# Up projection of a gated FFN: pairs of weight units against groups of four

## The chip, the core and the metric

The kernel runs on one core of one Trainium2 chip. The metric is device microseconds (us) of one execution. The kernel before takes 755.76 us, the median of three runs (755.01 to 755.77). All durations below come from one further execution that was recorded by the profiler; it took 755.7 us, of which 753.9 us lie between its first and its last instruction (the span). So 1.8 us lie around the span.

Engines are named as in the profile: PE does matrix products (PEld is its weight load), DVE is the vector engine, ACT the activation engine, POOL the general one, SP the queue that issues the transfers here. Each engine works through its own list of instructions in the order of the program.

## The reference, cut to what matters

Two decoder layers over 256 positions of width 1024. Each layer is an attention mixer followed by a gated feed-forward net (FFN) with a causal convolution of width 3:

```python
def conv_ffn(h, w_up, conv_w, conv_b, w_down):
    u = h @ w_up                                   # (256, 1024) @ (1024, 2 * 2816)
    up = jnp.pad(u, ((0, 0), (CONV_WIDTH - 1, 0), (0, 0)))
    uc = conv_b + sum(conv_w[j] * up[:, j:j + S] for j in range(CONV_WIDTH))
    gate, val = uc[..., :D_FF], uc[..., D_FF:]
    return (jax.nn.silu(gate) * val) @ w_down      # (256, 2816) @ (2816, 1024)
```

## The kernel before, in words

**Split numbers.** A product of 32-bit numbers is made of three products of rounded parts: high times high, high times rest, rest times high. Weights arrive as `raw` tiles. `Stream.start` has ACT write the high part (`whi`, L111), `Stream.finish` has DVE write the rest (`wlo`, L119). There are 6 `raw` buffers and 8 pairs of `whi` and `wlo`. A `raw` tile is loaded again (L83, on SP) once DVE has written the rest of the tile that held it; a pair of parts is written again once its unit was released (`Stream.release`) and PE is done with it.

**Units of the FFN.** 2816 gate columns and 2816 value columns are cut into blocks of 128. A block pair f (1 to 10; pair 0 is done apart by `first_up`) has four up units of 1024x128 weights: gate j=0 with e=0, 1, then value j=1 with e=0, 1. Below they are called f.1 to f.4. Each has 8 slices k.

**Up projection (`up`).** `xT[:, k]` holds, side by side, the high part and the rest of the input, 256 columns each. A wide product (L950) multiplies a slice of `whi` with all 512 columns; a narrow one (L968) multiplies the slice of `wlo` with the 256 high columns and adds to the second half. Per unit there are 8 wide and 8 narrow ones, all into one 128x512 accumulator, which fills a bank. Four banks rotate over the units (three named `acc`, one named `O`), so that a unit takes the bank of the unit four before it. In the kernel before, a pair of units (one j) is one piece of work: the first unit's 8 wide products, the second's first wide product, 8 narrow and 8 narrow, the second's other 7 wide.

**After a unit.** `join` adds the two halves of the accumulator: ACT copies the second half (L979), DVE adds it to the first and writes the sum to `sm` (L980). The bank is free once that addition has been made. `conv` makes the convolution of two joined units: two operations on ACT (L988), four on DVE (L991). For the gate a SiLU follows on ACT (L230 in the profile); for the value, DVE multiplies (L999), ACT takes the high part (`parts_of`, L1004) and DVE the rest (L230 on DVE).

**Down projection (`downs`).** A down unit b of 128x1024 weights takes 12 products of 128x512 (L1020 to L1022). Down units 2f-4 and 2f-3 are placed by `downs_after(f)`, from f=2 to f=9; six more come at the end of the FFN (`tail`).

**Turns.** `turn(fn)` writes one stretch of the program for all engines: up to two `start`s, then what is due under `first` (joins, SiLU, parts), one `finish`, what is due under `pre` (convolutions), the other `finish`es, then PE's work `fn`, then what is due under `post`. A join is due in the turn after its unit's, a gate's or value's convolution in the turn after its second unit's. Pair 0's convolutions are due one and three turns after the last `first_up` (`flip`, L932 to L940).

Of the kernel before, what the change touches and what calls it, by code (L numbers as in the profile page):

```python
# [10 lines left out]
F32 = mybir.dt.float32  # L11
# [6 lines left out]
P = 128  # L18
D = 1024
S = 256  # L20
# [123 lines left out]
def trunk_kernel(ctx, tc, x, a_w_qkv, a_w_o, b_w_qkv, b_w_o, ffn_norm, ffn_w_up, ffn_w_down, pack, mask_a, mask_b,  # L144
                 x_t, out):
    nc = tc.nc
    cp = ctx.enter_context(tc.tile_pool(name="cp", bufs=1))
    wp = ctx.enter_context(tc.tile_pool(name="wp", bufs=1))
    bp = ctx.enter_context(tc.tile_pool(name="bp", bufs=1))
# [5 lines left out]
    def qkv_cols(w, k0, nk, c0, n, stride):  # L155
        row = w.shape[1]
        return bass.AP(tensor=w.tensor, offset=w.offset + k0 * P * row + c0,
                       ap=[[row, P], [P * row, nk], [stride, n], [1, SW]])

    def qkv_units(w, ng):  # L160
        h3 = ng * NH * HD
        for sec in range(NSEC):
            opening = ng == 3 and sec == 0
            if opening:

                yield from (bass.AP(tensor=w.tensor, offset=w.offset + k * P * w.shape[1],
                                    ap=[[w.shape[1], P], [NH * HD, 2], [h3, 2], [1, SW]]) for k in range(8))
            for g in range(2 if opening else 0, ng):
                c0 = g * NH * HD + sec * SW
                yield from (qkv_cols(w, 2 * u, 2, c0, 2, h3) for u in range(4))  # L170
            c0 = 2 * h3 + sec * SW
            if ng == 3:
                yield from (qkv_cols(w, 2 * u, 2, c0, 2, NH * HD) for u in range(4))
                c0 += 2 * NH * HD

            if sec in V_TURN[ng]:
                yield from (qkv_cols(w, 2 * u, 2, 2 * h3 + (2 * NH * HD if ng == 3 else 0) + sec // 2 * 2 * SW, 2, SW)
                            for u in range(4))

    def out_units(w):  # L180
        wv = w.rearrange("(k p) n -> p k n", p=P)
        for n, u in OUT_UNITS:
            yield wv[:, 2 * u:2 * u + 2, n * 512:(n + 1) * 512]

    NPAIR = NFB // 2
    NT = 3

    def downs_after(f, j, e):

        bs = (2 * f - 4, 2 * f - 3)  # L190
        if not e or f not in range(2, NPAIR - NT + 2):
            return ()

        return bs[j:j + 1] if f > 2 else bs if j else ()

    def ffn_units(l):
        wu = ffn_w_up[l].rearrange("(k p) n -> p k n", p=P)
        wd = ffn_w_down[l].rearrange("(b p) n -> p b n", p=P)
        yield from (qkv_cols(ffn_w_up[l], 2 * u, 2, 0, 2, DFF) for u in range(4))
        for f in range(1, NPAIR):  # L200
            for j in range(2):
                for e in range(2):
                    c0 = j * DFF + (2 * f + e) * P
                    yield wu[:, :, c0:c0 + P]
                    for b in downs_after(f, j, e):
                        yield wd[:, b, :]
        for b in range(NFB - 2 * NT, NFB):
            yield wd[:, b, :]

    ws = Stream(nc, wp, [u for l, (q, ng, o) in enumerate(((a_w_qkv[0], NG, a_w_o[0]), (b_w_qkv[0], 1, b_w_o[0])))  # L210
                         for it in (qkv_units(q, ng), out_units(o), ffn_units(l)) for u in it])


    now = [0]
    first, pre, mid, post = {}, {}, {}, {}

    def at(table, dt, fn, *args):
        table.setdefault(now[0] + dt, []).append((fn, args))

    def turn(fn, pump=2, crowded=False):  # L220

        t = now[0]
        end = len(ws.parts) if t >= LATE else None
        n = min(pump, 1 if len(ws.parts) - ws.taken >= AHEAD else 2)
        if not crowded:
            ws.start(n)
        if t - 1 in EARLY_TURNS:
            ws.finish()
        for f, a in first.pop(t, ()):
            f(*a)  # L230
        ws.finish(1, end)
        for f, a in pre.pop(t, ()):
            f(*a)
        if crowded:
            ws.start(n)
        ws.finish(end=end)
        if fn is not None:
            fn()

        if t in EARLY_TURNS:  # L240
            ws.start(2)
        late = post.pop(t, [])
        part = PART[t >= PART_TURNS]
        late.sort(key=lambda fa: part.get(fa[0].__name__, len(part)))
        for f, a in late:
            f(*a)
        now[0] += 1
# [210 lines left out]
    def new_T():  # L458
        return cp.tile([P, 8, 2, S], F32R, name="xT", bufs=2)

    def new_acc():
        return ps.tile([P, 512], F32, name="acc", bufs=3)
# [439 lines left out]
    def ffn(xT, l, end):  # L902
# [41 lines left out]
        def up_bank():  # L944
            banks[0] += 1
            return ps.tile([P, 512], F32, name="O", bufs=1) if banks[0] % 4 == 2 else new_acc()

        def wide(acc, hi, ks):
            for k in ks:
                nc.tensor.matmul(acc, hi[:, k], xT[:, k].rearrange("p j t -> p (j t)"),  # L950
                                 start=(k == 0), stop=(k == 7 and ks[0] == 1))

        def up(f, j, e, st):


            def go():
                unit, = ws.take(1)
                if e == 0:
                    st["t"] = bp.tile([P, 512], F32, name="qk", bufs=5)
                    st["acc"] = bp.tile([P, 768], F32, name="sm", bufs=2)[:, 0:512]  # L960
                    st["up"] = up_bank(), up_bank()
                acc = st["up"][e]
                _, hi, lo = unit
                if e == 0:
                    wide(acc, hi, range(8))
                    wide(st["up"][1], ws.parts[ws.taken][0], range(1))
                for k in range(8):
                    nc.tensor.matmul(acc[:, S:2 * S], lo[:, k], xT[:, k, 0], start=False, stop=(k == 7 and e == 0))  # L968
                if e == 1:
                    wide(acc, hi, range(1, 8))  # L970
                ws.release(unit)
                at(first, 1, join, e, acc, st)
                if e == 1:
                    at(first if f == NPAIR - 1 and j else pre, 1, conv, f, j, st)
            return go

        def join(e, acc, st):
            small = bp.tile([P, 768], F32, name="pT", bufs=4)[:, 0:S]
# [31 lines left out]
        def down(b, c, ns=(0, 1), piece=None):  # L1010
            f, e = divmod(b, 2)
            cs = slice(e * S + c * P, e * S + (c + 1) * P)
            if not dacc:
                dacc.extend([ps.tile([P, 512], F32, name="S", bufs=4) for _ in range(2)] for _ in range(2))
            if b not in dw:
                dw[b] = ws.take(1)[0]
            _, hi, lo = dw[b]
            pieces = [(dacc[c][n], slice(n * 512, (n + 1) * 512), b == 0, b == NFB - 1 or (l, c, n, b) == PAUSE) for n in ns]
            for o, sl, start, stop in [piece] if piece else pieces:
                nc.tensor.matmul(o, acts[f][:, 0, cs], hi[:, sl], start=start, stop=False)  # L1020
                nc.tensor.matmul(o, acts[f][:, 1, cs], hi[:, sl], start=False, stop=False)  # L1021
                nc.tensor.matmul(o, acts[f][:, 0, cs], lo[:, sl], start=False, stop=stop)  # L1022
            if c == 1 and ns and ns[-1] == 1:
                ws.release(dw[b])

        def downs(b):
            def go():
                for c in range(2):
                    down(b, c)
            return go  # L1030
# [2 lines left out]
            for j in range(2):  # L1033
                turn(first_up(c, j), c + j)
        for f in range(1, NPAIR):
            for j in range(2):
                st = {}
                for e in range(2):
                    turn(up(f, j, e, st), 2)
                    for b in downs_after(f, j, e):  # L1040
                        turn(downs(b))
        rest = list(range(NFB - 2 * NT, NFB))

        def tail(c, bs, ns):
# [33 lines left out]
    xT = new_T()  # L1078
# [29 lines left out]
    xT = new_T()  # L1108
# [4 lines left out]
    def end0(c, n, acc):  # L1113
# [3 lines left out]
        if n == 1:  # L1117
            norms2[c].scale()
            if c == 0:
                at(post, 1, ready, norms2[0])  # L1120

    ffn(xT, 0, end0)


# [3 lines left out]
    xT = new_T()  # L1128
    out_proj(1, aT, xT)

    def end1(c, n, acc, c0=None):
# [3 lines left out]
        nc.sync.dma_start(out[0, c * P:(c + 1) * P, sl], xr[:, c, sl])  # L1135

    ffn(xT, 1, end1)


# [77 lines left out]
```

## Time and profile before

| what | value |
|---|---|
| median of three runs | 755.76 us |
| profiled execution, and its span | 755.7 us, 753.9 us |
| PE busy | 749.5 us, 99% of the span |
| DVE busy | 582.0 us, 77% |
| ACT busy | 506.4 us, 67% |
| POOL busy | 81.4 us, 11% |
| wide products (L950) | 640, into `acc` 118.8 us, into `O` 43.3 us |
| narrow products (L968) | 640, into `acc` 63.8 us, into `O` 22.6 us |
| rests of weights on DVE (L119) | 236, 283.8 us, 1218 ns each |
| high parts of weights on ACT (L111) | 236, 244.4 us, 1055 ns each |

Products are pipelined: the duration of one is longer than the time to the start of the next. So the pace of PE is read from starts. On DVE and ACT, too, the next operation may begin some 0.08 to 0.1 us before the former has ended, and lists are summed from start to start. The up projections of the first layer's pairs begin at 282.49 us, those of the second at 578.71 us.

### The profile page before, as it was taken

Reading aid. Unit: us, or ns where it says so; the run is one execution under the profiler, and the core shown is the slowest. Engines: PE = TensorE matmul, PEld = TensorE weight load, DVE = VectorE, ACT = ScalarE, POOL = GpSimd, SP = SyncE. Lnnn points to the kernel's source line nnn. Section 1 sums busy time; section 2 is a strip of 40 time slices with the busy share of each in tenths; the row PEclk is TensorE's granted clock in tenths of the full one; section 3 lists DMA queues with packets and bytes.
Section 4 is the critical chain, followed back from the end, with each engine's and each line's share of the span. In section 5 each row is a group of like instructions: output and inputs, shape, how many; then the busy total and the mean of one; then the engine's idle time right before and its main releaser. Section 6 shows DMA issues by size and latency. Waiting matters only on the chain.

```text
span 753.9 us, 12147 instructions
## 1 busy us (share of the span) xinstructions
PE 749.5 (99%) x4394; PEld 633.1 (84%) x4394; DVE 582.0 (77%) x1124; ACT 506.4 (67%) x887; POOL 81.4 (11%) x101
## 2 busy tenths in 40 slices
PE   9999999999999999999999999999999999999998
PEld 8888888888888888888888888888888888888886
DVE  7888786776686576997787786889866799877874
ACT  7878667677577457676656656787856667666660
POOL 0341331330131010000000001122000000000000
PEclk9999999999999999999999999999999999999999
DMA  9958576496456436587666663745545368666621
GB/s 294 333 145 285 158 259 233 149 294 219 132 194 230 128 94 201 152 249 217 195 188 181 194 193 113 250 140 155 161 136 166 112 198 243 201 185 197 194 95 56
DMA packets 151372, 141.69 MB, mean 188 GB/s; under 512 B 6288, under 2 KB 134928, under 8 KB 151312
## 3 DMA queue, kind: packets, MB, share of 16 engines
q1 hardware_dynamic: 148816, 130.96, 56.4%
q0 software_dynamic: 2496, 9.96, 3.5%
q8 instruction: 34, 0.56, 0.3%
q14 instruction: 26, 0.21, 0.1%
HBM read 131.99 MB, written 1.05 MB: 176 GB/s over the span
## 4 chain that ended last, share of the span: by engine, by line
PE 99%; DVE 0%; issue 0%
PE acc L950 15%; PE acc L467 13%; PE acc L469 13%; PE acc L468 13%; PE acc L968 8%; PE S L1021 5%; PE S L1022 5%; PE S L1020 5%; PE O L950 5%; PE O L968 3%; PE acc L524 2%; PE O L824 2%; PE S L791 2%; PE acc L600 1%; PE S L702 1%; PE S L469 1%
## 5 line engine op out<-in xcount | busy, mean ns | idle before, releaser
L119 DVE TENSOR_TENSOR wlo<-raw,whi 128x1024 fp32r<-128x1024 f32 x236 | 283.8, 1218 | 7.9 <-ACT whi L111 7.8
L111 ACT ACTIVATE whi<-raw 128x1024 fp32r<-128x1024 f32 x236 | 244.4, 1055 | 4.7 <-PE S L1021 1.4
L467 PE MATMUL acc<-whi,xT 128*128 128x512 f32 x424 | 171.1, 404 | 0.0
L469 PE MATMUL acc<-wlo,xT 128*128 128x512 f32 x424 | 165.6, 391 | 0.0
L468 PE MATMUL acc<-whi,xT 128*128 128x512 f32 x424 | 165.2, 390 | 0.0
L950 PE MATMUL acc<-xT,whi 128*128 128x512 f32 x480 | 118.8, 390 | 0.0
L950 PEld LDWEIGHTS acc<-xT,whi 128*128 128x128 f32 x480 | 88.8, 188 | 17.7
L469 PEld LDWEIGHTS acc<-wlo,xT 128*128 128x128 f32 x424 | 79.6, 188 | 17.3
L467 PEld LDWEIGHTS acc<-whi,xT 128*128 128x128 f32 x424 | 79.6, 188 | 15.9 <-issue 1.2
L468 PEld LDWEIGHTS acc<-whi,xT 128*128 128x128 f32 x424 | 79.8, 188 | 14.5
L1020 PE MATMUL S<-whi,kT 128*128 128x512 f32 x174 | 67.8, 390 | 0.0
L1021 PE MATMUL S<-whi,kT 128*128 128x512 f32 x174 | 67.8, 389 | 0.0
L1022 PE MATMUL S<-wlo,kT 128*128 128x512 f32 x174 | 67.7, 389 | 0.0
L327 POOL TENSOR_TENSOR rs_y<-rs_v,mhalf 128x8 f32<-128x8 f32 x32 | 53.1, 1659 | 128.1 <-DVE rs_v L325 128.1
L991 DVE SCALAR_TENSOR_TENSOR qk<-sm,taps,qk 128x255 f32<-128x255 f32 (+1 forms) x160 | 66.6, 477 | 0.4 <-ACT qk L988 0.4
L968 PEld LDWEIGHTS acc<-xT,wlo 128*128 128x128 f32 x480 | 62.9, 191 | 3.1
L968 PE MATMUL acc<-xT,wlo 128*128 128x256 f32 x480 | 63.8, 283 | 0.0
L980 DVE TENSOR_TENSOR sm<-acc,pT 128x256 f32<-128x256 f32 x60 | 25.4, 424 | 46.5 <-ACT pT L979 46.5
L988 ACT ACTIVATE qk<-sm,taps 128x256 f32<-128x256 f32 x80 | 47.9, 598 | 4.2 <-DVE sm L980 3.9
L950 PE MATMUL O<-xT,whi 128*128 128x512 f32 x160 | 43.3, 392 | 0.0
L1004 ACT ACTIVATE kT<-qk 128x512 fp32r<-128x512 f32 x22 | 13.9, 633 | 41.2 <-DVE qk L999 41.2
L555 DVE TENSOR_REDUCE qssq<-sq 128x8 f32<-128x512 f32 x32 | 21.8, 682 | 22.0 <-ACT sq L550 21.8
(171 smaller groups left out, 943.4 us busy)
## 6 DMA issues: line engine op xcount, KB each, us to landing
raw<-in_ffn_w_up_dram SPq DMA_DIRECT2D x80, 512.0 KB, 4.0
raw<-in_a_w_qkv_dram SPq DMA_DIRECT2D x144, 256.0 KB, 4.8
raw<-in_ffn_w_down_dram SPq DMA_DIRECT2D x44, 512.0 KB, 3.6
raw<-in_b_w_qkv_dram SPq DMA_DIRECT2D x48, 256.0 KB, 3.8
pL<-sm POOLq DMA_DIRECT2D x12, 384.0 KB, 4.6
raw<-in_a_w_o_dram SPq DMA_DIRECT2D x8, 512.0 KB, 4.3
raw<-in_ffn_w_up_dram SPq DMA_DIRECT2D x16, 256.0 KB, 4.5
raw<-in_b_w_o_dram SPq DMA_DIRECT2D x8, 512.0 KB, 4.1
```

Source lines behind the costliest of these rows:

```text
L111: self.nc.scalar.activation(hi, raw, AF.Copy)
L119: self.nc.vector.tensor_sub(lo, self.raw[self.done], r32(hi))
L327: nc.gpsimd.tensor_tensor(y, v, mhalf[:, 0:n], op=ALU.pow)
L467: nc.tensor.matmul(acc, T[:, k, 0, cs], hi, start=first, stop=False)
L468: nc.tensor.matmul(acc, T[:, k, 1, cs], hi, start=False, stop=False)
L469: nc.tensor.matmul(acc, T[:, k, 0, cs], lo, start=False, stop=last)
L950: nc.tensor.matmul(acc, hi[:, k], xT[:, k].rearrange("p j t -> p (j t)"), start=(k == 0), stop=(k == 7 and ks[0] == 1))
L968: nc.tensor.matmul(acc[:, S:2 * S], lo[:, k], xT[:, k, 0], start=False, stop=(k == 7 and e == 0))
L991: nc.vector.scalar_tensor_tensor(o[:, d:S], u[:, 0:S - d], cw[:, first_tap + b:first_tap + b + 1], o[:, d:S], op0=ALU.mult, op1=ALU.add)
L1020: nc.tensor.matmul(o, acts[f][:, 0, cs], hi[:, sl], start=start, stop=False)
L1021: nc.tensor.matmul(o, acts[f][:, 1, cs], hi[:, sl], start=False, stop=False)
L1022: nc.tensor.matmul(o, acts[f][:, 0, cs], lo[:, sl], start=False, stop=stop)
```

## The change

A pair f is now one group of four units with four turns: `one` (8 wide products of f.1, 4 of f.2), `two` (4 of f.2, the first of f.3 and of f.4, then the 8 narrow of f.1), `three` (the narrow ones of f.2, f.3 and f.4), `four` (the other 7 wide of f.3 and of f.4). `one` and `two` each take two units from the stream. A unit is released, and its join made due, when its last product has been written: f.1 after `two`, f.2 after `three`, f.3 and f.4 after `four`. The two down units of a pair come together behind the group, where the kernel before placed one behind each half (from f=3 on), and the weights are loaded in that order. The number of products, splits, joins, convolutions and transfers is the same, and so is the number of turns.

```diff
-    def downs_after(f, j, e):
-        bs = (2 * f - 4, 2 * f - 3)
-        if not e or f not in range(2, NPAIR - NT + 2):
-            return ()
-        return bs[j:j + 1] if f > 2 else bs if j else ()
+    def downs_after(f):
+        return (2 * f - 4, 2 * f - 3) if f in range(2, NPAIR - NT + 2) else ()
...
-                    for b in downs_after(f, j, e):
-                        yield wd[:, b, :]
+            for b in downs_after(f):
+                yield wd[:, b, :]
...
-        def wide(acc, hi, ks):
-            for k in ks:
-                nc.tensor.matmul(acc, hi[:, k], xT[:, k].rearrange("p j t -> p (j t)"),
-                                 start=(k == 0), stop=(k == 7 and ks[0] == 1))
-
-        def up(f, j, e, st):
-            def go():
-                unit, = ws.take(1)
-                if e == 0:
-                    st["t"] = bp.tile([P, 512], F32, name="qk", bufs=5)
-                    st["acc"] = bp.tile([P, 768], F32, name="sm", bufs=2)[:, 0:512]
-                    st["up"] = up_bank(), up_bank()
-                acc = st["up"][e]
-                _, hi, lo = unit
-                if e == 0:
-                    wide(acc, hi, range(8))
-                    wide(st["up"][1], ws.parts[ws.taken][0], range(1))
-                for k in range(8):
-                    nc.tensor.matmul(acc[:, S:2 * S], lo[:, k], xT[:, k, 0], start=False, stop=(k == 7 and e == 0))
-                if e == 1:
-                    wide(acc, hi, range(1, 8))
-                ws.release(unit)
-                at(first, 1, join, e, acc, st)
-                if e == 1:
-                    at(first if f == NPAIR - 1 and j else pre, 1, conv, f, j, st)
-            return go
+        def up(f):
+            units, accs, sts = [], [], ({}, {})
+
+            def wide(u, ks):
+                for k in ks:
+                    nc.tensor.matmul(accs[u], units[u][1][:, k], xT[:, k].rearrange("p j t -> p (j t)"),
+                                     start=(k == 0), stop=(k == 7 and u > 1))
+
+            def narrow(u):
+                for k in range(8):
+                    nc.tensor.matmul(accs[u][:, S:2 * S], units[u][2][:, k], xT[:, k, 0],
+                                     start=False, stop=(k == 7 and u < 2))
+                if u < 2:
+                    done(u)
+
+            def done(u):
+                j, e = divmod(u, 2)
+                ws.release(units[u])
+                at(first, 1, join, e, accs[u], sts[j])
+                if e == 1:
+                    at(first if f == NPAIR - 1 and j else pre, 1, conv, f, j, sts[j])
+
+            def begin(j):
+                units.extend(ws.take(2))
+                sts[j]["t"] = bp.tile([P, 512], F32, name="qk", bufs=5)
+                sts[j]["acc"] = bp.tile([P, 768], F32, name="sm", bufs=2)[:, 0:512]
+                accs.extend((up_bank(), up_bank()))
+
+            def one():
+                begin(0)
+                wide(0, range(8))
+                wide(1, range(4))
+
+            def two():
+                begin(1)
+                wide(1, range(4, 8))
+                wide(2, range(1))
+                wide(3, range(1))
+                narrow(0)
+
+            def three():
+                for u in (1, 2, 3):
+                    narrow(u)
+
+            def four():
+                for u in (2, 3):
+                    wide(u, range(1, 8))
+                    done(u)
+
+            return one, two, three, four
...
         for f in range(1, NPAIR):
-            for j in range(2):
-                st = {}
-                for e in range(2):
-                    turn(up(f, j, e, st), 2)
-                    for b in downs_after(f, j, e):
-                        turn(downs(b))
+            for fn in up(f):
+                turn(fn, 2)
+            for b in downs_after(f):
+                turn(downs(b))
```

**On PE, pairs 1 and 2 of the first layer.** Between pairs 1 and 2 there is no down unit, before and now. `whi_3391`, `whi_3394` and the next two are units 2.1 to 2.4; the accumulator named first is the bank. In the kernel before, from the end of pair 1:

```order
L950 MATMUL acc_3482<-xT_2983,whi_3371 128x512 x7
L950 MATMUL acc_3554<-xT_2983,whi_3391 128x512 [waits DVE_49]
L950 MATMUL O_3555<-xT_2983,whi_3394 128x512 [waits DVE_49]
L968 MATMUL acc_3554<-xT_2983,wlo_3392 128x256 x8
L968 MATMUL O_3555<-xT_2983,wlo_3395 128x256 x8
L950 MATMUL O_3555<-xT_2983,whi_3394 128x512 x7
L950 MATMUL acc_3617<-xT_2983,whi_3430 128x512 [waits DVE_49]
L950 MATMUL acc_3618<-xT_2983,whi_3463 128x512 [waits DVE_49]
L968 MATMUL acc_3617<-xT_2983,wlo_3431 128x256 x8
```

and in the changed kernel, from the end of pair 1:

```order
L950 MATMUL acc_3445<-xT_2983,whi_3368 128x512 x7
L950 MATMUL acc_3446<-xT_2983,whi_3371 128x512 x7
L950 MATMUL acc_3560<-xT_2983,whi_3391 128x512 [waits DVE_49]
L950 MATMUL O_3561<-xT_2983,whi_3394 128x512 [waits DVE_49]
L950 MATMUL O_3561<-xT_2983,whi_3394 128x512 x7
L950 MATMUL acc_3584<-xT_2983,whi_3425 128x512 [waits DVE_49]
L950 MATMUL acc_3585<-xT_2983,whi_3428 128x512 [waits DVE_49]
L955 MATMUL acc_3560<-xT_2983,wlo_3392 128x256 x8
L955 MATMUL O_3561<-xT_2983,wlo_3395 128x256 x8
```

The first product into the third bank (`acc_3617`, now `acc_3584`) waits for DVE's addition of the unit that had the bank before, 1.3. It now stands behind 16 wide products of pair 2, where it stood behind 16 wide and 16 narrow ones; and unit 1.3 is now finished (the first row) only after all narrow ones of pair 1.

**On DVE, from the join of unit 1.1 or 1.2 to those of 1.3 and 1.4.** `acc_3405`, `O_3406` and then `acc_3481`, `acc_3482` (now `acc_3445`, `acc_3446`) are the banks of units 1.1 to 1.4; `qk<-S` is a convolution of pair 0, `qk<-sm` one of pair 1. In the kernel before:

```order
L980 TENSOR_TENSOR sm_3404<-O_3406,pT_3467 128x256
L119 TENSOR_TENSOR wlo_3431<-raw_3349,whi_3430 128x1024
L991 SCALAR_TENSOR_TENSOR qk_3403<-sm_3404,taps_123,qk_3403 128x255 x2
L991 SCALAR_TENSOR_TENSOR qk_3403<-sm_3404,taps_123,qk_3403 128x254 x2
L980 TENSOR_TENSOR sm_3480<-acc_3481,pT_3504 128x256
L119 TENSOR_TENSOR wlo_3464<-raw_3375,whi_3463 128x1024
L991 SCALAR_TENSOR_TENSOR qk_3429<-S_3300,taps_123,qk_3429 128x255 x2
L991 SCALAR_TENSOR_TENSOR qk_3429<-S_3300,taps_123,qk_3429 128x254 x2
L999 TENSOR_TENSOR qk_3428<-qk_3428,qk_3429 128x512
L980 TENSOR_TENSOR sm_3480<-acc_3482,pT_3538 128x256
```

and in the changed kernel:

```order
L999 TENSOR_TENSOR sm_3404<-acc_3405,pT_3465 128x256
L119 TENSOR_TENSOR wlo_3426<-raw_3349,whi_3425 128x1024
L119 TENSOR_TENSOR wlo_3429<-raw_3375,whi_3428 128x1024
L999 TENSOR_TENSOR sm_3404<-O_3406,pT_3501 128x256
L119 TENSOR_TENSOR wlo_3462<-raw_3398,whi_3461 128x1024
L1010 SCALAR_TENSOR_TENSOR qk_3424<-S_3300,taps_123,qk_3424 128x255 x2
L1010 SCALAR_TENSOR_TENSOR qk_3424<-S_3300,taps_123,qk_3424 128x254 x2
L1018 TENSOR_TENSOR qk_3423<-qk_3423,qk_3424 128x512
L1010 SCALAR_TENSOR_TENSOR qk_3403<-sm_3404,taps_123,qk_3403 128x255 x2
L1010 SCALAR_TENSOR_TENSOR qk_3403<-sm_3404,taps_123,qk_3403 128x254 x2
L999 TENSOR_TENSOR sm_3444<-acc_3445,pT_3541 128x256
L999 TENSOR_TENSOR sm_3444<-acc_3446,pT_3544 128x256
```

The addition for unit 1.1 used to stand ahead of all this and now opens it. Between it and the addition for 1.3 stand three rests of weights, the addition for 1.2, two convolutions and a product; both additions for 1.3 and 1.4 now come together at the end.

**On ACT, the same stretch of the changed kernel:**

```order
L111 ACTIVATE whi_3425<-raw_3349 128x1024
L111 ACTIVATE whi_3428<-raw_3375 128x1024
L1007 ACTIVATE qk_3423<-S_3299,taps_123 128x256 x2
L111 ACTIVATE whi_3461<-raw_3398 128x1024
L226 ACT_TABLE_LOAD
L226 ACTIVATE qk_3423<-qk_3423 128x512
L998 ACTIVATE pT_3465<-acc_3405 128x256
```

Before, the copy for unit 1.1 (`pT<-acc_3405`) stood ahead of pair 0's first convolution and ahead of the high part of 2.4; now both of these, the table load and the SiLU stand ahead of the copy, because the unit is finished a turn later.

## The prediction

> **What bounds the kernel now.** I read the page first: busy times, then the clock, then the chain that ended last; after it the table of waits for PE.
>
> ```profile
> span 753.9 us, 12147 instructions
> PE 749.5 (99%) x4394; PEld 633.1 (84%) x4394; DVE 582.0 (77%) x1124; ACT 506.4 (67%) x887; POOL 81.4 (11%) x101
> PEclk9999999999999999999999999999999999999999
> PE 99%; DVE 0%; issue 0%
> ```
>
> ```profile
> PE S L275 <- DVE qk L272: 1.0, 1, 1.0
> ```
>
> PE is busy all the time, its clock row shows no slice under 9 tenths, the chain is PE's own list, and its only wait is 1.0 us at the start. So the change can gain only by closer spacing of products, and loses whatever wait it puts in. Next comes PE's timeline around the first pairs; columns are start, length, line, tiles, count.
>
> ```profile
> 282.49 1.98 PE L950 MATMUL acc<-xT,whi 128*128 128x512 f32 x8
> ...
> 285.48 0.60 PE L936 MATMUL S<-ident,qk 128*128 128x128 f32 x4
> 285.83 1.20 PE L968 MATMUL O<-xT,wlo 128*128 128x256 f32 x8
> ...
> 299.62 2.21 PE L950 MATMUL acc<-xT,whi 128*128 128x512 f32 x9
> 301.67 2.08 PE L968 MATMUL acc<-xT,wlo 128*128 128x256 f32 x16
> 303.58 1.78 PE L950 MATMUL acc<-xT,whi 128*128 128x512 f32 x7
> 305.19 0.39 PE L1020 MATMUL S<-whi,kT 128*128 128x512 f32 x1
> ...
> 319.00 2.20 PE L950 MATMUL acc<-xT,whi 128*128 128x512 f32 x9
> 321.04 2.08 PE L968 MATMUL acc<-xT,wlo 128*128 128x256 f32 x16
> ```
>
> From start to start, 9 wide products take 2.04 us (319.00 to 321.04), 0.227 each; 16 narrow ones 1.91 (301.67 to 303.58), 0.119 each. Seven wide ones behind a narrow run take 1.61 (303.58 to 305.19) where seven at 0.227 are 1.59: a run of narrow products costs 0.02 us behind it. Four transposes take 0.35 (285.48 to 285.83).
>
> DVE's timeline shows how near the first pairs stand to a wait.
>
> ```profile
> 287.90 1.64 DVE L991 SCALAR_TENSOR_TENSOR qk<-S,taps,qk 128x255 f32<-128x255 f32 x4
> ...
> 291.85 0.42 DVE L980 TENSOR_TENSOR sm<-O,pT 128x256 f32<-128x256 f32 x1 [1.18 <-ACT pT L979]
> ...
> 300.83 0.42 DVE L980 TENSOR_TENSOR sm<-acc,pT 128x256 f32<-128x256 f32 x1 [0.97 <-ACT pT L979]
> 301.17 1.22 DVE L119 TENSOR_TENSOR wlo<-raw,whi 128x1024 fp32r<-128x1024 f32 x1
> 302.30 1.66 DVE L991 SCALAR_TENSOR_TENSOR qk<-sm,taps,qk 128x255 f32<-128x255 f32 x4
> 304.00 0.69 DVE L999 TENSOR_TENSOR qk<-qk 128x512 f32<-128x512 f32 x1
> 304.60 0.69 DVE L230 TENSOR_TENSOR kT<-qk,kT 128x512 fp32r<-128x512 f32 x1
> ```
>
> The addition at 300.83 is that of unit 1.4; it ends at 301.25. The ninth product of the row at 299.62, at 301.43, is the first into that bank again (unit 2.4). So 0.18 us are left there today: the additions of pair 1 decide when pair 2 may go on.
>
> **The change part by part.**
>
> *Spacing.* 20 narrow runs per layer (10 pairs, two halves; 40 in all) become 10. 20 runs fewer at 0.02 us: -0.4 us. If a run of 32 left more behind it than one of 16, the other 20 runs would give back the same 0.02 each at most twice, so the term lies between 0 and -0.4. I take -0.4.
>
> *The wait for banks in pair 2.* PE needs the bank of unit 1.3 for unit 2.3's first product, which now stands, counted from unit 1.1's first one, behind 48 wide products (12, 6, 14, 16 of `one`, `two`, `four`, then `one` and a third of `two`), 32 narrow ones and 4 transposes: 48 x 0.227 + 32 x 0.119 + 0.35 = 15.1 us. In the first layer it is due at 282.49 + 15.1 = 297.6.
>
> When is the bank free? ACT's rows, and the transfer of unit 2.4's weights (its issue, and the answer on transfers, where the last column is us to landing):
>
> ```profile
> 283.18 2.95 ACT L111 ACTIVATE whi<-raw 128x1024 fp32r<-128x1024 f32 x3
> ...
> 286.29 1.02 ACT L988 ACTIVATE qk<-S,taps 128x256 f32<-128x256 f32 x2
> ...
> 289.62 1.28 ACT L230 ACT_TABLE_LOAD   x1 [1.37 <-DVE qk L991]
> 290.92 0.63 ACT L230 ACTIVATE qk<-qk 128x512 f32<-128x512 f32 x1
> 291.45 0.36 ACT L979 ACTIVATE pT<-O 128x256 f32<-128x256 f32 x1
> ```
>
> ```profile
> 280.39 0.37 SPq L83 DMA_DIRECT2D raw<-in_ffn_w_up_dram  x1
> ```
>
> ```profile
> raw<-in_ffn_w_up_dram SPq DMA_DIRECT2D x1, 512.0 KB, 6.2
> ```
>
> In turn `two` of pair 1 ACT now splits 2.3 and 2.4 ahead of pair 0's first convolution. The weights of 2.4 land at 280.39 + 6.2 = 286.6 (that transfer's loads are the same as before). One split later (0.95 from start to start, three in 2.95) the convolution's two operations start at 287.55 and take 1.02; DVE's four follow within 0.05 and take 1.65: 290.3. Table load to SiLU 1.30 (289.62 to 290.92), SiLU to copy 0.53, copy to addition 0.40 (291.45 to 291.85): the addition of 1.1 starts at 292.6. Nothing of pair 1's PE work is late for it.
>
> From there DVE's list runs without a gap to the addition of 1.3, by the rows from 300.83 on: addition 0.34, two rests 2.26, addition 0.34, rest 1.13, convolution 1.70, product 0.60, convolution 1.66, together 8.0: 300.6. The last of these is pair 1's own gate; its SiLU stands ahead of the copies on ACT, so 0.1 + 0.53 + 0.40 follow, and the addition takes 0.42: the bank is free at 302.1. PE waits **4.5 us**, and 0.1 more for 1.4's bank, whose addition starts 0.34 after 1.3's where PE needs it 0.23 later. What goes is the spread of the joins: those of 1.3 and 1.4 are now due together, behind three convolutions.
>
> The second layer has one split more done by then, and its transfer lands earlier:
>
> ```profile
> 578.71 1.98 PE L950 MATMUL acc<-xT,whi 128*128 128x512 f32 x8
> ```
>
> ```profile
> 579.40 2.00 ACT L111 ACTIVATE whi<-raw 128x1024 fp32r<-128x1024 f32 x2
> ```
>
> ```profile
> 575.53 0.37 SPq L83 DMA_DIRECT2D raw<-in_ffn_w_up_dram  x1
> ```
>
> ```profile
> raw<-in_ffn_w_up_dram SPq DMA_DIRECT2D x1, 512.0 KB, 4.3
> ```
>
> Landed at 579.8, it holds nothing up: three splits run from 579.40, the convolution starts at 582.25, DVE is done with it at 585.0, the addition of 1.1 starts at 587.3 (+2.3), that of 1.3 is done at 587.3 + 8.0 + 1.45 = 596.8. PE is due at 578.71 + 15.1 = 593.8: **3.0 us**, and 0.1.
>
> Bounds: if the transfer did not hold up the first layer, ACT would start the convolution 0.6 earlier, the wait being 3.9; if the transfers behind it (now issued some 2.5 us earlier, since 2.1's rest is) slowed it by as much, 5.1. Hand-offs of 0.05 to 0.1, of which each chain has six, give 0.3 either way in each layer.
>
> *Later pairs.* From pair 2 on, two down units follow each group. The additions of f.3 and f.4 come in the first of them; their banks are needed after both (24 products, 5.4 us), `one` (2.7) and 4 wide ones (0.9). DVE's work in a group and two down units is 6 rests (6.8), 4 additions (1.4), two convolutions (3.3), product and rest of the parts (1.2): 12.7 of PE's 16.5 us. After PE's wait DVE is ahead, and I count nothing. Units wait for release longer (f.1's until `two`), which lets ACT run 4 to 6 units ahead in place of 5; the splits stand one per turn as before. The six rests behind a pair are the same six, so SP's transfers, which wait for them, keep their pace. At the end of the FFN the join of 10.3 can run under 10.4's seven wide products, so pair 10's chain gets no longer.
>
> *The sum.* 753.9 - 0.4 + 4.6 + 3.1 = 761.2 of span, with 1.8 around it **763.0 us**. The profiled execution (755.7) stands within 0.1 of the median of runs, so no more is corrected.
>
> *The clock after a wait.* The opening is the one place where the trace shows PE after idle time:
>
> ```profile
> 4.48 2.05 PE L524 MATMUL acc<-whi,xT 128*128 128x512 f32 x4
> ...
> 8.39 1.07 PE L524 MATMUL acc<-whi,xT 128*128 128x512 f32 x4
> ```
>
> The same four products take 2.05 and then 1.07 us. The clock row has no slice under 9 there, so it doesn't tell. A wait of 4.6 us could bring that back; between nothing and some 7 products at twice their 0.227 I put 0 to 1.6 us on each wait, and take nothing, as the row of the clock shows no drop.
>
> The Trainium skill (TensorE: Matmul & The Clock Gate, Part 1) states that PE falls to half its clock after an idle window of about 3.4 us, and needs as long a busy one to come back. By that rule the first wait could, and the second could not, drop the clock; half speed over 3.4 us would be 1.7 us, an estimate from that page. No run here shows it.
>
> **The rivals.**
>
> *The clock drops.* As forecast, and then the products behind one wait (or both) run at the opening's pace: +1.6, 764.6. For it: the opening. Against: 4.6 us of idleness may be too short, and no row shows it.
>
> *The rests come late, not the banks.* In pair 3 the rest of the third unit is now due 4 us earlier. Its fourth place among the splits belongs to this row:
>
> ```profile
> 317.14 1.22 DVE L119 TENSOR_TENSOR wlo<-raw,whi 128x1024 fp32r<-128x1024 f32 x1
> ```
>
> It ends at 318.4. Pair 3 starts behind two down units from the row at 305.19 on, at 305.19 + 24 x 0.227 = 310.6 before and now, and the changed order needs the fourth rest after `one`, `two` and two of the three narrow runs of `three`, 2.72 + 2.32 + 1.91 later, at 317.6: 0.8 late in each layer. Alone, without the banks' wait: 753.9 - 0.4 + 1.6 + 1.8 = 756.9. For it: DVE is late there today, too. Against: PE's wait for the banks comes first and gives DVE 3 us or more, so that beside it the rests cost nothing.
>
> *No wait (the other side: not slower).* One mechanism, ACT and DVE: if the copy for 1.1 were made before SiLU and table load, or the additions for 1.3 and 1.4 ahead of the convolutions, the bank would be free by 297.6 and the half of the narrow runs that goes would be all: 755.3. It decides if the chain above is 4.5 us shorter. Against it: the order of the lists, and the 0.18 us that are left today.
>
> **How the numbers follow.** Forecast 0.75 (763.0), clock 0.14 (764.6), no wait 0.06 (755.3), rests alone 0.05 (756.9). Under 0.2%, 1.5 us, a run cannot be told from no change here; no wait (-0.4) and rests alone (+1.2) lie within it. So slower 0.89; within 0.2% 0.09; faster 0.02, what a gain of 1.5 us from spacing alone would need, four times the term. The range: the bounds of the waits, 0.6 from the transfer and 0.3 from the hand-offs of each layer, and 0.4 for the spacing give 761.8 to 764.6, where one dropped clock lies, too; the runs shown spread by 0.8 (755.01 to 755.77), so I give 761.0 to 765.5. The two cases outside hold 0.11.
>
> **What would show it.** Right: two waits of PE in the table, on L950's first product into an `acc` bank, released by DVE's addition, 4.5 us near 297.6 and 3.0 near 593.8; DVE without a gap in the 8 us before; no wait after pair 2. Seven wide products behind the narrow run of 32 at 1.61. Wrong: the same waits in later pairs (the two down units don't cover), a wait for a rest (L955 as the waiter), or products at 0.4 us behind the waits.

## The result, and the profile after

The changed kernel takes 765.73 us (median of 4 runs, 765.63 to 765.76), the kernel before 755.41 us beside it (4 runs): ratio 1.0135, interval 1.0122 to 1.0147. It is slower, as forecast, but by 10.3 us where 7.3 were forecast; 765.73 stands 2.7 us above the forecast of 763.0 and 0.2 us beyond the range.

The page of the changed kernel, in the lines that answer to those of before:

```profile
span 763.9 us, 12267 instructions
PE 752.2 (98%) x4394; PEld 635.0 (83%) x4394; DVE 580.2 (76%) x1124; ACT 506.1 (66%) x887; POOL 81.2 (11%) x101
PEclk9999999999999999999999999999999999999999
PE 93%; DVE 3%; ACT 2%; DMA 1%; issue 1%; SPq 0%; ACTq 0%
```

The chain no longer runs on PE alone. The table of waits for PE (us in total, times, longest; the second row is the wait at the start, and a third, not shown here, has 0.2 us in the opening):

```profile
PE acc L950 <- DVE sm L999: 7.0, 2, 4.3
PE S L271 <- DVE qk L268: 1.1, 1, 1.1
```

Two waits, on a wide product, released by DVE's addition: the forecast's two. Its timeline around both, first and second layer:

```profile
295.65 2.11 PE L950 MATMUL O<-xT,whi 128*128 128x512 f32 x8
302.11 1.22 PE L950 MATMUL acc<-xT,whi 128*128 128x512 f32 x2 [4.35 <-DVE sm L999]
303.12 1.91 PE L955 MATMUL acc<-xT,wlo 128*128 128x256 f32 x8
304.84 1.38 PE L955 MATMUL O<-xT,wlo 128*128 128x256 f32 x8
306.05 2.08 PE L955 MATMUL acc<-xT,wlo 128*128 128x256 f32 x16
307.96 3.36 PE L950 MATMUL acc<-xT,whi 128*128 128x512 f32 x14
...
597.85 1.98 PE L950 MATMUL O<-xT,whi 128*128 128x512 f32 x8
602.51 1.22 PE L950 MATMUL acc<-xT,whi 128*128 128x512 f32 x2 [2.69 <-DVE sm L999]
603.53 1.91 PE L955 MATMUL acc<-xT,wlo 128*128 128x256 f32 x8
605.24 1.37 PE L955 MATMUL O<-xT,wlo 128*128 128x256 f32 x8
606.45 2.08 PE L955 MATMUL acc<-xT,wlo 128*128 128x256 f32 x16
608.37 2.00 PE L950 MATMUL acc<-xT,whi 128*128 128x512 f32 x8
```

In the first layer the waiting product starts at 302.11; the sum of the lists said 302.1. It was due at 297.6 (the row at 295.65, of whose eight products one came 0.1 late), so the wait is 4.5. In the second it was due at 597.85 + 8 x 0.227 = 599.7 and starts at 602.51, a wait of 2.85. What follows is new. The two wide and 32 narrow products behind each wait take 5.85 us (302.11 to 307.96; 602.51 to 608.37 gives 5.86), where 2 x 0.227 + 32 x 0.119 are 4.27: 1.6 us too long, twice. These 1.6 us hold the wait for 1.4's bank, which the forecast had as 0.1. Eight narrow products take 1.72 (303.12 to 304.84), 0.215 each in place of 0.119. The 16 at 306.05 are at 0.119 again.

The view by stretches gives the granted clock (after the engines' busy times come clock, share of the transfer engines and GB/s), of a stretch ahead of the first wait, of the ones behind the two waits, and of a later one:

```profile
290.60:294.00 3.40, 3.40 (x17) 2.81 (x16) 2.22 (x3) 3.39 (x6) 0.00 (x0) 1.00 0.35 103
302.10:305.30 3.20, 3.19 (x13) 3.06 (x14) 3.17 (x7) 2.02 (x3) 0.00 (x0) 0.50 0.24 52
602.50:605.70 3.20, 3.19 (x13) 3.05 (x14) 3.17 (x7) 2.03 (x3) 0.00 (x0) 0.50 0.23 87
613.00:616.00 3.00, 3.00 (x15) 2.49 (x14) 1.97 (x5) 2.62 (x6) 0.00 (x0) 1.00 0.77 220
```

In the 3.2 us shown behind each wait PE ran at half its clock. The clock record in the trace dates the two falls: from 302.01 to 305.42 and from 602.38 to 605.80, 3.41 us each, beginning 0.1 us before PE goes on. The row of 40 slices on the profile's page (19 us each) shows 9 in every slice all the same, since 3.4 of 19 us at half speed leave 0.91.

The additions on DVE, and ahead of them the split of 2.4 and the table load on ACT, stand as the lists said:

```profile
292.57 0.43 DVE L999 TENSOR_TENSOR sm<-acc,pT 128x256 f32<-128x256 f32 x1 [1.18 <-ACT pT L998]
...
301.63 0.76 DVE L999 TENSOR_TENSOR sm<-acc,pT 128x256 f32<-128x256 f32 x2 [1.03 <-ACT pT L998]
```

```profile
286.61 1.06 ACT L111 ACTIVATE whi<-raw 128x1024 fp32r<-128x1024 f32 x1 [0.74 <-DMA raw<-in_ffn_w_up_dram]
...
290.34 1.28 ACT L226 ACT_TABLE_LOAD   x1 [0.82 <-DVE qk L1010]
```

The addition of 1.1 starts at 292.57 (forecast 292.6), those of 1.3 and 1.4 follow together at 301.63, and the split of 2.4 did wait for its transfer until 286.61.

### The profile page after: what moved, and what is told of

Same layout as the page of the kernel before. It is cut to its first block, busy times and chain, and to the rows that moved or that the text cites. A ratio compares the mean times of both kernels' runs of the same rounds, so it can differ in the third digit from the quotient of the medians.

```text
span 763.9 us, 12267 instructions
## 1 busy us (share of the span) xinstructions
PE 752.2 (98%) x4394; PEld 635.0 (83%) x4394; DVE 580.2 (76%) x1124; ACT 506.1 (66%) x887; POOL 81.2 (11%) x101
## 4 chain that ended last, share of the span: by engine, by line
PE 93%; DVE 3%; ACT 2%; DMA 1%; issue 1%; SPq 0%; ACTq 0%
PE acc L463 13%; PE acc L950 13%; PE acc L465 12%; PE acc L464 12%; PE acc L955 7%; PE S L1041 5%; PE S L1039 5%; PE S L1040 5%; PE O L950 4%; PE O L955 2%; PE O L820 2%; PE acc L520 2%; PE S L787 2%; PE acc L596 1%; PE S L698 1%; DVE qk L1010 1%
## 5 line engine op out<-in xcount | busy, mean ns | idle before, releaser
L999 DVE TENSOR_TENSOR sm<-acc,pT 128x256 f32<-128x256 f32 x60 | 23.7, 421 | 63.2 <-ACT pT L998 63.1
L955 PE MATMUL acc<-xT,wlo 128*128 128x256 f32 x480 | 65.6, 287 | 0.0
L1007 ACT ACTIVATE qk<-sm,taps 128x256 f32<-128x256 f32 x80 | 45.9, 598 | 10.4 <-DVE sm L999 10.3
L998 ACT ACTIVATE pT<-acc 128x256 f32<-128x256 f32 x60 | 20.4, 372 | 31.1 <-PE acc L955 31.0
L950 PE MATMUL O<-xT,whi 128*128 128x512 f32 x160 | 40.2, 391 | 0.0
```

The source lines that it names most:

```text
L950: nc.tensor.matmul(accs[u], units[u][1][:, k], xT[:, k].rearrange("p j t -> p (j t)"), start=(k == 0), stop=(k == 7 and u > 1))
L955: nc.tensor.matmul(accs[u][:, S:2 * S], units[u][2][:, k], xT[:, k, 0], start=False, stop=(k == 7 and u < 2))
```

## The experiments

The theory: the loss is two waits for banks between pairs 1 and 2, as forecast, and a fall of PE's clock behind each, which the forecast had left out. Rivals: the 2.7 us beyond the forecast lie elsewhere (in rests of weights that come late, or in later groups), or the waits have another cause than the order of DVE's and ACT's lists.

**PE kept busy while it waits.** In `two` of pair 2, ahead of the product that waits:

```diff
                 wide(1, range(4, 8))
+                if f == 2:
+                    spare = ps.tile([P, 512], F32, name="S", bufs=4)
+                    for _ in range((19, 12)[l]):
+                        nc.tensor.matmul(spare, units[0][1][:, 0], xT[:, 0].rearrange("p j t -> p (j t)"),
+                                         start=True, stop=True)
```

> The changed kernel, with PE kept busy while it waits: 19 wide products into an unused bank in the first layer (4.3 us), 12 in the second (2.7 us), each ahead of the product that waits; their results are not used. Banks come free at the same time. If the 2.7 us beyond the forecast are PE's clock, which falls while it waits: granted clock 1.000, products behind the wait at 0.227 and 0.120, and 765.7 - 2 x 1.6 = 762.5 us. If they lie elsewhere: 765.7.

Measured: 762.58 us (762.37 to 762.98), 3.15 less than the changed kernel, with 31 products more. PE's timeline in the first layer:

```profile
297.50 4.47 PE L984 MATMUL S<-xT,whi 128*128 128x512 f32 x19
302.00 0.83 PE L950 MATMUL acc<-xT,whi 128*128 128x512 f32 x2
302.67 1.12 PE L955 MATMUL acc<-xT,wlo 128*128 128x256 f32 x8
303.63 1.12 PE L955 MATMUL O<-xT,wlo 128*128 128x256 f32 x8
304.59 2.08 PE L955 MATMUL acc<-xT,wlo 128*128 128x256 f32 x16
306.51 3.36 PE L950 MATMUL acc<-xT,whi 128*128 128x512 f32 x14
```

The bank comes free at nearly the same time (302.00, before 302.11), and the narrow products behind it are at 0.120 (302.67 to 303.63). So what lies beyond the forecast was the clock: it falls because PE is idle, not because of what it waits for. And 762.58 is within 0.4 us of the forecast (763.0), which added nothing for the clock. The 2 wide and 32 narrow products take 4.51 us here (302.00 to 306.51), 0.2 above 4.27, as the second wide one waits for 1.4's bank. So the clock's own part of the 5.85 us is 1.35 per wait.

**Other banks for units 1.3 and 1.4.** Two banks of the four that the down projection will use stand idle during pairs 1 and 2:

```diff
-                accs.extend((up_bank(), up_bank()))
+                if f == 1 and j == 1:
+                    accs.extend(ps.tile([P, 512], F32, name="S", bufs=4) for _ in range(2))
+                else:
+                    accs.extend((up_bank(), up_bank()))
```

> The changed kernel, but units 1.3 and 1.4 of each layer write to two banks that stand unused until the first down unit, so that units 2.3 and 2.4 need not wait for their joins. If the two waits for banks and the slow products behind them are the whole loss: no wait on L950, and 755.4 - 0.4 = 755.0 us. The next to come late is the rest of pair 0's activations (the last DVE operation ahead of the first down unit), which by the lists is ready 1.2 us after PE's need in the first layer and in time in the second: then 756.2. If the loss has another place, about 765.

Measured: 756.32 us (median of 11 runs), ratio to the kernel before 1.0013 (1.0005 to 1.0022). No wait for a bank is left; PE's table has one new line:

```profile
PE S L1043 <- DVE kT L226: 1.0, 1, 1.0
```

It is the second product of the first down unit, in the first layer, and DVE's rows ahead of it are these:

```profile
303.77 1.66 DVE L1013 SCALAR_TENSOR_TENSOR qk<-sm,taps,qk 128x255 f32<-128x255 f32 x4
305.47 0.69 DVE L1021 TENSOR_TENSOR qk<-qk 128x512 f32<-128x512 f32 x1
306.08 0.69 DVE L226 TENSOR_TENSOR kT<-qk,kT 128x512 fp32r<-128x512 f32 x1
```

The rest of pair 0's activations ends at 306.77 and PE goes on at 306.82, 1.1 later than it could. So the waits for banks, with the clock that falls behind them, were nearly the whole loss, and DVE's lateness in this stretch shows at the next place that needs it, 1.2 us as summed.

**Joins ahead of SiLU and parts.** One line of `turn`, in the changed kernel:

```diff
-        for f, a in first.pop(t, ()):
+        for f, a in sorted(first.pop(t, ()), key=lambda fa: getattr(fa[0], "__name__", "") != "join"):
             f(*a)
```

> The changed kernel, with the joins ahead of SiLU and of the parts of activations in every turn's list. By the summed lists the addition of 1.1 starts 1.3 us earlier in the first layer, and no SiLU stands ahead of the copies for 1.3 and 1.4 (1.0 us): the waits shrink from 4.5 to 2.3 us and from 2.9 to 0.4 us. 755.4 - 0.4 + 2.7 = 757.7 us, and 1.6 more (759.3) if PE's clock falls after 2.3 us, too. If the waits come from PE finishing 1.3 and 1.4 late and not from what stands ahead of their joins: 765.7.

Measured: 757.45, 757.63, 759.29 and 759.51 us, in two pairs, with a mean granted clock of 1.000 in the lower pair and 0.998 in the upper one. Both numbers of the expectation came true, each in half of the runs. The profiled execution is one of the upper pair:

```profile
299.92 1.13 PE L950 MATMUL acc<-xT,whi 128*128 128x512 f32 x2 [2.17 <-DVE sm L999]
300.84 1.91 PE L955 MATMUL acc<-xT,wlo 128*128 128x256 f32 x8
```

and in the view by stretches, behind the place of the first wait and of the second:

```profile
299.90:303.20 3.30, 3.28 (x14) 3.04 (x15) 3.27 (x7) 2.29 (x4) 0.00 (x0) 0.54 0.47 162
597.60:600.90 3.30, 3.30 (x25) 3.03 (x25) 3.27 (x8) 2.36 (x4) 0.00 (x0) 1.00 0.21 57
```

The wait for 1.3's bank is 2.3 us in place of 4.5, and next to nothing in the second layer. So what stands ahead of the joins sets the waits. And a wait of 2.3 us lets the clock fall in two runs of four.

**Pairs 1 and 2 in the order of before**, groups of four from pair 3 on (`up_old` is `up` of the kernel before; its lines are left out):

```diff
-            for fn in up(f):
-                turn(fn, 2)
+            if f < 3:
+                for j in range(2):
+                    st = {}
+                    for e in range(2):
+                        turn(up_old(f, j, e, st), 2)
+            else:
+                for fn in up(f):
+                    turn(fn, 2)
```

> Pairs 1 and 2, between which no down unit stands, in the order of before; groups of four from pair 3 on (16 narrow runs fewer instead of 20). If the loss lies between pairs 1 and 2 alone: no wait, 755.4 - 0.3 = 755.1 us. If the groups also need the rests of weights too early in pair 3, where DVE is late: two waits of a narrow product for a rest, 0.8 us in the first layer and 0.5 in the second, 756.4 us. If later groups lose as well: above 757.

Measured: 756.61 us (median of 11 runs), ratio 1.0015 (1.0006 to 1.0024). The new line of PE's table and the two places in its timeline:

```profile
PE acc L984 <- DVE wlo L119: 0.9, 2, 0.6
```

```profile
318.14 1.10 PE L984 MATMUL acc<-xT,wlo 128*128 128x256 f32 x7 [0.57 <-DVE wlo L119]
...
614.74 1.22 PE L984 MATMUL acc<-xT,wlo 128*128 128x256 f32 x8 [0.35 <-DVE wlo L119]
```

By the spacing of products the two waits are 0.73 and 0.51 us, where 0.8 and 0.5 were expected. (The table also has 0.6 us in the opening, on L520, where other kernels have between nothing and 0.3.) So a narrow product does wait for a rest of pair 3, as the prediction's second rival says, but only in this kernel. In the changed kernel it is not the wait for banks that hides it. With the spare banks, where no wait for a bank is left, the fourth rest of pair 3 (counting PE's units and DVE's rests in order) and the first product that needs it are these:

```profile
314.72 1.22 DVE L119 TENSOR_TENSOR wlo<-raw,whi 128x1024 fp32r<-128x1024 f32 x1
```

```profile
319.16 1.12 PE L955 MATMUL O<-xT,wlo 128*128 128x256 f32 x8
```

The rest is done at 315.94, 3.2 us early (3.5 in the second layer). There it stands ahead of pair 2's last convolution in DVE's list; with pairs 1 and 2 in the old order it stands behind it. No group from pair 4 on waits in this kernel, and none from pair 3 on in the changed one: its loss lies between pairs 1 and 2.

**Both cures.** The spare banks and the joins first, together (both edits above in one kernel):

> Both cures at once: spare banks for units 1.3 and 1.4, and joins ahead of SiLU and parts. The chain of DVE is 1.3 us shorter, so that pair 0's rest of activations is ready in time, too: no wait is left, and the spacing of products shows alone. If half the narrow runs are worth 0.4 us: 755.0 us, 0.4 below the kernel before. If a run of 32 narrow products leaves more behind it than one of 16: 755.4. If the rests of pair 3 come late (as in the kernel with pairs first): a wait of up to 1.2 us and 756.

Measured: 755.16 us (median of 11 runs) beside 755.66, ratio 0.9993 (0.9984 to 1.0002). PE waits for nothing behind the start, so the rests of pair 3 are not late here either (the fourth is ready 4.6 us early in the first layer). Its timeline of pair 2 in the first layer:

```profile
298.02 3.04 PE L955 MATMUL acc<-xT,wlo 128*128 128x256 f32 x24
300.89 1.12 PE L955 MATMUL O<-xT,wlo 128*128 128x256 f32 x8
301.85 1.78 PE L950 MATMUL acc<-xT,whi 128*128 128x512 f32 x7
303.47 1.75 PE L950 MATMUL O<-xT,whi 128*128 128x512 f32 x7
```

Seven wide products behind 32 narrow ones take 1.62 (301.85 to 303.47), as long as behind 16 before (1.61). So half the runs should be worth the 0.4 us; the measured gain of 0.5 agrees, but its interval holds 1, so the times do not show a gain. The traces do: added from each product's start to the next start on PE, the 1280 products of the up projections take 222.83 us in the kernel before, 222.47 with both cures and 222.49 with the spare banks. It is the fastest of the kernels tried, by a margin that the times cannot tell from none.

**Parts of the wait filled.** The kernel with PE kept busy, with 11 and 7 products in place of 19 and 12:

```diff
-                    for _ in range((19, 12)[l]):
+                    for _ in range((11, 7)[l]):
```

> The changed kernel with PE kept busy for part of its waits: 11 wide products in the first layer and 7 in the second, so that 2.0 and 1.3 us of idleness are left. If PE's clock falls only after 3.4 us of idleness, or after more than 2.3: granted clock 1.000 in every run and 762.5 us. If it falls, in some runs, after shorter waits, too: 764.1 in the runs with one fall, 765.7 with two, and products at 0.43 and 0.21 us behind a wait.

and with 8 and 4:

```diff
-                    for _ in range((19, 12)[l]):
+                    for _ in range((8, 4)[l]):
```

> As the one before, with 8 and 4 wide products: 2.7 and 1.9 us of idleness are left. If a wait of 2.3 us lets the clock fall in about half of the runs (as with the joins first) and longer ones more often: one fall in most runs, 764.1 us, none or two in the others. If only waits over 3.4 us did: 762.5 us in all.

Measured, with the waits as PE's spacings show them in the profiled execution:

| kernel | idle left, first and second layer | times of the runs, us | falls of the clock |
|---|---|---|---|
| 19 and 12 products | about 0.2, about 0.2 | 762.37, 762.44, 762.71, 762.98 | none |
| 11 and 7 | 1.95, 1.3 | 762.57, 762.79, 763.13, 764.49 | one in one run of four |
| joins first | 2.3, 0.1 | 757.45, 757.63, 759.29, 759.51 | one in two of four |
| 8 and 4 | 2.7, 1.9 | 762.84, 764.24, 764.59, 765.87 | none, one, one, two |
| the changed kernel | 4.5, 2.85 | 765.63, 765.72, 765.73, 765.76 | two in each |

Falls are counted from the steps of the times (1.4 to 1.9 us each) and agree with the mean granted clock of each run: 0.999 or 1.000 without one, 0.997 or 0.998 with one, 0.995 or 0.996 with two. The profiled execution with 11 and 7 has the fall behind a wait of 1.95 us, and only after some faster products:

```profile
297.68 2.65 PE L984 MATMUL S<-xT,whi 128*128 128x512 f32 x11
302.12 0.83 PE L950 MATMUL acc<-xT,whi 128*128 128x512 f32 x2 [1.79 <-DVE sm L1004]
302.79 1.36 PE L955 MATMUL acc<-xT,wlo 128*128 128x256 f32 x8
303.96 1.91 PE L955 MATMUL O<-xT,wlo 128*128 128x256 f32 x8
```

Eight narrow products take 1.17 at first and 1.70 then. Behind waits below 2 us the clock fell in one run of four with 11 and 7 products, and in at least one with 8 and 4 (the run with two falls has one behind its wait of 1.9 us); behind the changed kernel's 2.85 us it fell every time. But for the wait of 4.5 us, none of these waits had the 3.4 us that the Trainium skill (TensorE: Matmul & The Clock Gate, Part 1) states for an idle window. A fall cost much the same each time: the 34 products take 5.85 to 5.98 us behind a wait with a fall and 4.49 to 4.51 behind one without.

The clock record in the traces shows more than chances. All falls in the profiled executions, but for one in each after PE's last product (idle: the stretch less the time of the products in it, at 0.227 and 0.120 us each):

| kernel and wait | clock at half, from and to | PE idle in the 3.41 us ahead of the fall |
|---|---|---|
| changed kernel, first layer | 302.01, 305.42 | 3.4 |
| changed kernel, second | 602.38, 605.80 | 2.7 |
| joins first, first | 300.17, 303.59 | 2.35 |
| 11 and 7, first | 303.45, 306.87 | 2.15 |
| 8 and 4, first | 302.16, 305.58 | 2.7 |

Each lasts 3.41 us and begins 86 or 87 times 3.413 us after the clock last rose: the first of the changed kernel 296.96 us (87 x 3.413) after the rise at 5.05 us in its opening, the second 296.96 us after 305.42. The falls after the last products lie on the same count. So in these executions the clock changes only at the ends of fixed stretches of 3.41 us, and it fell where PE had been idle for 2.15 us or more of one. The idlest stretches without a fall hold 1.95 us (8 and 4, second layer, 599.12 to 602.54) and 1.5 (11 and 7, second layer). A wait that the end of a stretch cuts in two counts in parts, and the rise in the opening lies between 4.3 and 7.0 us in the nine executions. That would make waits of 2 to 3 us a matter of chance, as in the table above; it is read from these traces, and no run was made to test it.

## Why the prediction was wrong in size

*Spacing, -0.4.* Right: seven wide products cost the same behind 32 narrow ones as behind 16, and all products of the up projections together take 0.36 us less in the trace of the kernel with both cures than in that of the kernel before. The times alone (0.5 us less, within the interval) would not show it.

*The waits for banks, 4.6 and 3.1.* Right, place, releaser and size: 4.5 and 2.85 measured for 1.3's bank (4.5 and 3.0 forecast), about 0.2 for 1.4's where the clock holds (0.1 forecast), and the additions behind which PE waits stand within 0.1 us of the summed lists in the first layer. Filling the wait, taking the need for the bank away and moving the joins up all did what this part says.

*Later pairs, nothing.* Right. No group behind pair 2 waits in the changed kernel, and none from pair 4 on in any other.

*The clock after a wait.* This step failed. It bounded the cost at 0 to 1.6 us on each wait and then took nothing, "as the row of the clock shows no drop"; the products behind both waits took 1.6 us longer, 1.35 of it by the clock. With the waits as measured and these 1.6 the sum is 753.9 - 0.4 + 4.5 + 2.85 + 3.2 + 1.8 = 765.85, against 765.73. There were two faults in it. The clock row of the kernel before could not speak on this, because PE never waited there behind the start. And the view by stretches gives 1.00 even for the opening, where the products took twice as long: the clock record of that trace begins with the rise to full clock at 6.82 us, and the time ahead of it is counted as full. So the only row that bore on the question was the opening, and it spoke for a fall; the step put it into a rival and nothing into the sum. The second fault: the second wait was thought too short; by the Trainium skill (TensorE: Matmul & The Clock Gate, Part 1) an idle window of about 3.4 us is needed, and here 2.85 us were enough in four runs of four. Half speed lasted 3.41 us each time, as the 3.4 that the Trainium skill states there for the way back.

*The rivals.* The clock's fall was a rival with a chance of 0.14 and one fall in its price; it happened, twice. The rests that come late were priced from their place in the list of the kernel before; in the changed order they stand earlier and are 3 to 7 us ahead of their need even where no bank is waited for, so this rival was no threat to the changed kernel. The kernel without a wait did not happen. The kernel with both cures, at 755.16, bears out its price of 755.3, but not the first of its two conditions: with the copy for 1.1 ahead of SiLU and table load (joins first), 2.3 us of the first layer's wait are left. Its second condition, the additions ahead of the convolutions, was not tried.

*The range* left out two falls, which lay inside the step's own bounds (2 x 1.6): to hold them it had to reach 766.2.

## What to carry to other kernels

Where work is regrouped, list for each buffer the operation that frees it and what now stands ahead of that operation in its engine's own list: two additions that moved behind three convolutions cost 7 us of waits here, on engines that were 77% and 67% busy. A wait of PE can cost more than its length: here waits of 2 to 2.7 us slowed the products behind them in some executions and waits of 2.85 and 4.5 us in all, by about 1.4 us each time. So give such a wait a term of its own in the sum, with a chance, and not nothing. And read the granted clock over a stretch as short as the wait itself, since a slice of 19 us hides it.

## What the hardware showed that was not expected

PE's clock fell to half after waits of 1.95 us (one run of four), 2.3 us (two of four) and 2.85 us (four of four), for 3.41 us and some 1.35 to 1.5 us of time each, and filling the wait with products whose results nobody uses prevented it: 3.15 us less for 31 products more. After the shortest of the waits with a fall in a trace (1.95 us) it came only 1.3 us after PE had gone on (302.12, 303.45). The falls and rises lie whole multiples of 3.413 us apart, and in the traces a fall came where PE had been idle 2.15 us or more of such a stretch, none where it had been idle 1.95 or less.
